# Lower products of an expert pair between gate and up of the next pair, with groups pinned in order and a branch hint

## The chip, the cores and the metric

The kernel runs on one core of one Trainium2 chip. The metric is the device time of one execution in microseconds. Smaller is better. Three executions of the kernel before gave 1344.26, 1339.33 and 1338.83 us, a median of 1339.33 us.

## What is computed

Two transformer blocks follow each other on 256 tokens of width 1024, all in float32. Each ends in a mixture of experts: every token goes to two experts, and each expert multiplies by three weight matrices.

```python
# first block: 16 experts of inner width 256
for e in range(N_EXPERTS):
    act = jax.nn.silu(t @ w_gate[e]) * (t @ w_up[e]) * gates[:, e:e + 1]
    y = y + act @ w_down[e]
...
# second block: 32 experts of inner width 512
for e in range(N_EXPERTS_2):
    a = jax.nn.silu(tok @ w_gate[e]) * (tok @ w_up[e])
    out = out + combine[:, e:e + 1] * (a @ w_down[e])
...
x = x + g2 * hier_moe_2(h2, ...)
return rms_norm_2(x, final_norm_g)
```

Between the two expert layers stands the mixer of the second block (projections, two scans, and their merge), which the change does not touch.

## The kernel before

`moe` (L937) is called twice, for 16 experts of width 256 (L1468, "first layer") and for 32 of width 512 (L1968, "second layer"). Experts are taken in **pairs**, which sit side by side on TensorE: each expert has 64 places for its tokens, and the two experts of a pair fill two halves of 64 columns. Four experts, two pairs, are a **quad**.

The steps of a pair, by the names of their PSUM tiles, are these. *gate*: 16 products into `pgg` (second layer) or the first half of `pgu` (first layer), with SiLU on ACT (`sgm`, L1159) and DVE (L1160). *up*: 16 products into `pgu`, then `act` on DVE (L1161). *turn* (L1165): transposes of `act` into `pactT`, copied to `actT` by ACT (L1170). *down* (L1173): the lower products into two tiles `pdn`, then `Pg`, `Ph`, `Pl` on DVE and ACT. *combine* (L1193): eight products `py` that add the pair into the sum `y`. Once for each quad *dispatch* (L1092) collects the tokens of the next quad: 32 products `pgx`, whose results ACT copies to `XT`, and then `pgt` and `pws`; `places` (L1085) makes its selection `Dd` on DVE just ahead.

In the loop (L1229 to L1247) `gate_up` runs gate and up of pair p; between the two, `half` (L1212) combines pair p-2 and turns pair p-1. Then `lower` (L1225) runs down of pair p-1, and `dispatch` follows at the end of a quad. The framework's scheduler sets the final order within each engine; `issue_after` pins an instruction behind another on its engine, and before the change only `half` of the first layer is pinned in the loop.

The weights come through one queue, SP, in the order that `Stream` writes (L504): gate and up of pair p, then down of pair p-1. Each load is 1024 KB, four for each matrix of a pair in the second layer and two in the first. A load needs a free buffer of a pool with 19 (`NG`), and it waits in SP's queue until the last product of the buffer's former tenant is done. `take` sets how far loads are written ahead (8 loads). The last two loads of the second layer are cut in halves (L534 to L542).

Behind the last pair every engine reads how many further chunks of tokens there are (`ns`, L1253), and branches past their code (`tc.If(ns > j)`, L1262). In these inputs no chunk is left, in either layer, and the branch is taken over the whole body.

Of the kernel before, what the change touches and what calls it, by code (L numbers as in the profile page):

```python
# [15 lines left out]
ALU = mybir.AluOpType  # L16
# [6 lines left out]
KD = 8  # L23
# [24 lines left out]
H1 = 1  # L48
# [74 lines left out]
def _body(es, tc, I, cst_d, msk_d, out_d, tap, stop):  # L123
# [380 lines left out]
    class Stream:  # L504
# [9 lines left out]
        def add_pair(self, a, b):  # L514
            p = len(self.ap)
            self.ap[p] = {k: (self.load(a, k), self.load(b, k)) for k in "gud"}
            keys = []
            for k in "gud":
                for i in range(len(self.ap[p][k][0])):
                    keys += [(p, k, 0, i), (p, k, 1, i)]  # L520
            gu = [q for q in keys if q[1] != "d"]
            d = [q for q in keys if q[1] == "d"]
            tail = self.order[len(self.order) - self.nd:] if self.order else []
            if p and self.n <= len(self.order) - len(tail):
                self.order[len(self.order) - len(tail):] = gu + tail + d
            else:
                self.order += gu + d
            self.nd = len(d)
# [16 lines left out]

        def take(self, p, kinds, look=8):
            want = [q for q in self.order if q[0] == p and q[1] in kinds]
            self.ahead(max(self.order.index(q) for q in want) + 1 + look)
            out = [[[self.t[(p, k, s, i)] for i in range(len(self.ap[p][k][s]))] for s in range(2)] for k in kinds]
            return out if kinds == "gu" else out[0]  # L550

# [384 lines left out]

    def moe(x, E, router, gcol, bcol, st, FE, n_static, mid=None, before_if=None, gate=None, idle=None):  # L937
        epg = E // 4
# [23 lines left out]
        y = [[ax_ps("py") for _ in range(2)] for _ in range(2)]  # L962
        if gate is not None:
# [70 lines left out]
        if gate is not None:  # L1034
# [57 lines left out]
        def dispatch(e0, n, xt=None, d=None, late=None):  # L1092
# [8 lines left out]
            for kk in range(4):  # L1101
# [6 lines left out]
                for j in range(2):  # L1108
                    k = 2 * kk + j
                    if late is not None and j:  # L1110
                        if bcol is None:
# [28 lines left out]

        def gate_up(gu, xt, off, wcol, half=None):
            act = W("act", [FE])
            if FE == 256:
                p = mm_ps("pgu", (2, 256))
                outs = [p[:, 0, :], p[:, 1, :]]
            else:
                outs = [mm_ps("pgg"), mm_ps("pgu")]
            for o, ws in zip(outs, gu):
                for k in range(KD):
                    for s in range(2):  # L1150
                        pc = ws[s]
                        per = KD // len(pc)
                        mm(o[64 * s:64 * s + 64, :], xt[:, k, off + 64 * s:off + 64 * s + 64], pc[k // per][:, k % per, :],
                           k == 0, k == KD - 1)
                if half:
                    half()
                    half = None
            sg = W("sgm", [FE])
            A.activation(sg, outs[0], AF.Sigmoid)  # L1159
            V.tensor_tensor(sg, sg, outs[0], op=ALU.mult)  # L1160
            V.scalar_tensor_tensor(act.rearrange("p (f c) -> p c f", f=NF), sg.rearrange("p (c f) -> p c f", f=NF), wcol,  # L1161
                                   outs[1].rearrange("p (c f) -> p c f", f=NF), op0=ALU.mult, op1=ALU.mult)
            return act

        def turn(act):  # L1165
            p = mm_ps("pactT", (NF, 128))
            for f in range(NF):
                PE.transpose(p[:, f, :], act[:, 128 * f:128 * f + 128], ident)
            aT = W("actT", [NF, 128])
            A.activation(aT, p, AF.Copy)  # L1170
            return aT

        def down(dn, aT):  # L1173
            parts = []
            for n in range(2):
                q = mm_ps("pdn")
                for f in range(NF):
# [4 lines left out]
                if gate is not None:  # L1182
                    qg = W("Pg", [512])
                    V.tensor_tensor(qg, q, gate[:, n, :], op=ALU.mult)  # L1184
                    q = qg
# [7 lines left out]
        def combine(parts, gt, first, final):  # L1193
            for n in range(2):
                for i in range(2):
                    for m in range(2):
                        mm(y[i][n], gt[:, 128 * i:128 * i + 128], parts[n][m], first and m == 0, final and m == 1)

# [10 lines left out]
        ei = spill()  # L1209
        acts, sums = [], []  # L1210

        def half():  # L1212
            with after(t2["mm"]) if E == 16 and H1 else nullcontext():
                if sums:
                    combine(*sums.pop(0))
                if acts:
                    acts[0][1] = turn(acts[0][1])

# [6 lines left out]
        def lower():  # L1225
            p, aT, gt = acts.pop(0)
            sums.append((down(st.take(p, "d"), aT), gt, p == 0 and gate is None, p == last - 1))

        for qi, e0 in enumerate(quads):  # L1229
            n = min(4, E + n_static - e0)  # L1230
            xt, gt, ws = nxt
            for a in range(n // 2):
# [6 lines left out]
                ahead = a == n // 2 - 1 and qi + 1 < len(quads)  # L1239
                if ahead:  # L1240
                    nn = min(4, E + n_static - e0 - 4)
                    d = places(e0 + 4, nn)
                if acts:
                    lower()
                if ahead:
                    nxt = dispatch(e0 + 4, nn, d=d)
                acts.append([p, act, gt[:, a, :]])  # L1247
        half()
        lower()
        half()  # L1250
        if before_if:
# [7 lines left out]
        def nest(j):  # L1259
            if j >= NSPILL:  # L1260
                return
            with tc.If(ns > j):  # L1262
                if not held:
# [4 lines left out]
                for k in "gud":  # L1268
                    out[k] = [[], []]
                    for i in range(len(aps[k][0])):  # L1270
                        for s in range(2):
# [6 lines left out]
                            q += 1  # L1278
                act = gate_up([out["g"], out["u"]], xt, 0, ws[:, 0:1])
                combine(down(out["d"], turn(act)), gt[:, 0, :], False, True)  # L1280
# [686 lines left out]

    y = moe(x3, 32, rt, mod2q, sh2q, st2, 512, 0, gate=gf[0], idle=last_ada)  # L1968
    ss = S("sf", [2, 2], bufs=1)
# [41 lines left out]
```

## Time and profile before

| | us |
|---|---|
| median of three executions | 1339.33 |
| the profiled execution | 1341.91 |
| its span, first to last instruction | 1340.14 |
| first expert layer, first gate product to last combine | 174.4 to 316.0 |
| second expert layer, first gate product to last combine | 862.9 to 1325.8 |

The profile is one execution. Busy time is not speed: a matmul is pipelined, so the next one starts before the modelled end of the last, and the pace of a group is read from the starts of the groups. "PE" is TensorE's products, "PEq" its sequencer. The idle time in square brackets is that of the engine just before the row, with what ended it. The trace counts each float32 product of 512 or 256 columns of gate, up and down as two instructions, so 16 products are 32 there.

### The profile page before, as it was taken

To read this page: it belongs to the slowest core of one execution; us is meant where nothing else is said; L and a number is where in the kernel's file an instruction comes from. 1 tells how busy PE (TensorE), PEld (TensorE's weight loads), DVE (VectorE), ACT (ScalarE), POOL (GpSimd) and SP (SyncE) were. 2 spreads that over 40 slices of the span, in tenths; PEclk is the share of its full clock that TensorE was granted. 3 is DMA by queue.
4 is the path that set the end of the run, shared out by engine and by line. 5 is a ranking of instruction groups with operands and counts; after the bars stand their busy time and mean duration, and the time that the engine had idled before them with its cause. 6 is when DMAs were issued, how large, how long until landed. Compare 5 with 4: busy or idle time off the path is not lost. (4 is left out here: it accounts for less than half of the span.)

```text
span 1340.1 us, 19921 instructions
## 1 busy us (share of the span) xinstructions
PE 1278.2 (95%) x8098; PEld 842.5 (63%) x8098; DVE 647.4 (48%) x1416; ACT 437.5 (33%) x756; POOL 38.7 (3%) x50
## 2 busy tenths in 40 slices
PE   6988999998999999999999999899999999999995
PEld 5845466666788998898988988643434334343431
DVE  6895541115479988876565765821111111211113
ACT  5734322223234655554344443310201111110102
POOL 4110100000000000000000000100000000000000
PEclk9989999998999999999999999899999999999998
DMA  8698789963423231342516677699999999999990
GB/s 272 232 338 316 253 333 380 410 282 117 153 82 95 77 112 50 114 131 81 164 44 206 228 263 286 238 422 421 422 422 422 422 421 421 422 422 422 421 391 33
DMA packets 124356, 359.81 MB, mean 268 GB/s; under 512 B 15272, under 2 KB 64593, under 8 KB 97632
## 3 DMA queue, kind: packets, MB, share of 16 engines
q1 hardware_dynamic: 114224, 355.49, 69.8%
q10 hardware_dynamic: 9024, 2.24, 0.8%
q8 instruction: 68, 1.11, 0.3%
q0 software_dynamic: 1008, 0.70, 0.2%
q14 instruction: 32, 0.26, 0.1%
HBM read 357.35 MB, written 1.05 MB: 267 GB/s over the span
## 5 line engine op out<-in xcount | busy, mean ns | idle before, releaser
L156 PE MATMUL pg<-hT,hi 128*128 128x256 f32 (+1 forms) x1024 | 232.7, 321 | 1.5 <-DVE Qg L1352 1.5
L156 PE MATMUL pgu<-w,XT 128*64 128x256 f32 (+1 forms) x1088 | 190.3, 481 | 0.0
L156 PE MATMUL pdn<-w,actT 128*64 128x512 f32 x656 | 180.6, 596 | 0.5 <-ACT actT L1170 0.5
L156 PEld LDWEIGHTS pg<-hT,hi 128*128 128x128 f32 x1024 | 167.2, 188 | 16.3 <-DVE Qg L1352 1.7
L236 DVE TENSOR_TENSOR lo<-w,hi 128x1024 fp32r<-128x1024 f32 x122 | 146.0, 1219 | 49.6 <-ACT hi L235 21.5
L156 PE MATMUL pg<-hT,lo 128*128 128x256 f32 (+1 forms) x512 | 162.3, 317 | 0.0
L235 ACT ACTIVATE hi<-w 128x1024 fp32r<-128x1024 f32 x122 | 125.0, 1053 | 93.4 <-PE pr L156 32.1
L156 PEld LDWEIGHTS pgu<-w,XT 128*64 128x64 f32 x1088 | 81.3, 137 | 92.2 <-issue 71.4
L156 PE MATMUL pgg<-w,XT 128*64 128x512 f32 x512 | 127.1, 596 | 0.0
L156 PEld LDWEIGHTS pdn<-w,actT 128*64 128x64 f32 x656 | 56.0, 137 | 93.9 <-issue 85.7
L156 PEld LDWEIGHTS pg<-hT,lo 128*128 128x128 f32 x512 | 96.2, 188 | 7.4 <-issue 0.4
L156 PE MATMUL pr<-hi,hT 128*128 128x256 f32 (+1 forms) x384 | 90.6, 326 | 3.7 <-PEq L1262 3.7
L156 PEld LDWEIGHTS pgg<-w,XT 128*64 128x64 f32 x512 | 37.8, 137 | 70.5 <-issue 68.7
L1184 DVE TENSOR_TENSOR Pg<-pdn,g 128x512 f32<-128x512 f32 x32 | 22.1, 689 | 117.5 <-PE pdn L156 117.3
L1160 DVE TENSOR_TENSOR sgm<-sgm,pgg 128x512 f32<-128x512 f32 x16 | 11.0, 688 | 130.6 <-ACT sgm L1159 130.6
L1188 ACT ACTIVATE Ph<-Pg 128x512 fp32r<-128x512 f32 x32 | 20.1, 629 | 163.5 <-DVE Pg L1184 163.5
L156 PEld LDWEIGHTS pr<-hi,hT 128*128 128x128 f32 x384 | 65.2, 191 | 10.5 <-issue 4.1
L1161 DVE SCALAR_TENSOR_TENSOR act<-sgm,ws,pgu 128x512 f32<-128x512 f32 (+1 forms) x25 | 23.8, 952 | 87.2 <-PE pgu L156 86.8
L156 PE MATMUL pr<-lo,hT 128*128 128x256 f32 (+1 forms) x192 | 62.6, 326 | 0.0
L1119 ACT ACTIVATE XT<-pgx,adaq,mod2q 128x256 f32<-128x256 f32 x60 | 30.0, 562 | 96.3 <-PE pgx L156 96.3
L156 PE MATMUL pgx<-Dd,xnh 128*128 128x256 f32 (+1 forms) x208 | 53.0, 295 | 3.9 <-DVE Dd L1089 3.8
L156 PEld LDWEIGHTS pgx<-Dd,xnh 128*128 128x128 f32 x208 | 40.3, 195 | 20.4 <-issue 13.7
(520 smaller groups left out, 1920.0 us busy)
## 6 DMA issues: line engine op xcount, KB each, us to landing
w<-in_w_gate_dram SPq DMA_DIRECT2D x82, 1024.0 KB, 16.5
w<-in_w_up_dram SPq DMA_DIRECT2D x82, 1024.0 KB, 12.6
w<-in_w_down_dram SPq DMA_DIRECT2D x80, 1024.0 KB, 16.3
w<-in_w_in_dram SPq DMA_DIRECT2D x98, 512.0 KB, 4.5
w<-in_w_ada_dram SPq DMA_DIRECT2D x24, 1024.0 KB, 6.4
w<-in_w_out_dram SPq DMA_DIRECT2D x4, 1024.0 KB, 5.2
w<-in_w_branch_b_dram SPq DMA_DIRECT2D x8, 512.0 KB, 4.5
w<-in_w_branch_a_dram SPq DMA_DIRECT2D x8, 512.0 KB, 4.6
```

The lines of the kernel that those rows point to most:

```text
L156: t2["mm"] = PE.matmul(out, lhsT, rhs, start=start, stop=stop, skip_group_check=True)
L235: t2["hi"] = A.activation(hi[:, ks], t, AF.Copy)
L236: t2["lo"] = V.tensor_tensor(lo[:, ks], t, hi[:, ks].bitcast(F32), op=ALU.subtract)
L1119: A.activation(xt[:, k, 0:w], p[:, j, :], AF.Identity, scale=gcol[:, k:k + 1], bias=bcol[:, k:k + 1])
L1160: V.tensor_tensor(sg, sg, outs[0], op=ALU.mult)
L1161: V.scalar_tensor_tensor(act.rearrange("p (f c) -> p c f", f=NF), sg.rearrange("p (c f) -> p c f", f=NF), wcol, outs[1].rearrange("p (c f) ...
L1184: V.tensor_tensor(qg, q, gate[:, n, :], op=ALU.mult)
L1188: A.activation(ph, q, AF.Copy)
```

## The change

`gate_up` is split into `gate` and `up`, with their common loop in `up_to`. `lower` turns pair p-1 and runs its down between gate and up of pair p, and combine of pair p-1 follows up of pair p. Gate, up, turn, the first half of down, combine and dispatch are each pinned behind the product issued last before them. Down's loads move from behind up to between gate and up, and `take` writes 12 loads ahead in the second layer and 10 in the first. In the second layer every dispatch, not only the first, gives every second `XT` copy to DVE. Combine's loops change places, so that both products with `Ph` stand ahead of those with `Pl`. A hint on TensorE's queue ahead of the last turn names the branch at `ns` as likely taken. The argument `gate` of `moe` becomes `gain`.

```diff
         def add_pair(self, a, b):
...
-            gu = [q for q in keys if q[1] != "d"]
-            d = [q for q in keys if q[1] == "d"]
+            g, u, d = ([q for q in keys if q[1] == k] for k in "gud")
...
-                self.order[len(self.order) - len(tail):] = gu + tail + d
+                self.order[len(self.order) - len(tail):] = g + tail + u + d
...
-        def take(self, p, kinds, look=8):
...
+            self.ahead(max(self.order.index(q) for q in want) + 1 + (12 if n > 1 else 10))
...
-                    if late is not None and j:
+                    if (late is not None or E == 32) and j:
...
+        def gate(w, xt, off):
...
+            with after(t2["mm"]):
+                up_to(outs[0], w, xt, off)
             sg = W("sgm", [FE])
             A.activation(sg, outs[0], AF.Sigmoid)
             V.tensor_tensor(sg, sg, outs[0], op=ALU.mult)
+            return sg, outs[1]
...
         def turn(act):
             p = mm_ps("pactT", (NF, 128))
-            for f in range(NF):
-                PE.transpose(p[:, f, :], act[:, 128 * f:128 * f + 128], ident)
+            with after(t2["mm"]):
+                for f in range(NF):
+                    tr = PE.transpose(p[:, f, :], act[:, 128 * f:128 * f + 128], ident)
+            t2["mm"] = tr
...
         def lower():
-            p, aT, gt = acts.pop(0)
-            sums.append((down(st.take(p, "d"), aT), gt, p == 0 and gate is None, p == last - 1))
+            p, a, gt = act
+            return down(st.take(p, "d"), turn(a)), gt, p == 0 and gain is None, p == last - 1
...
-                act = gate_up(st.take(p, "gu"), xt, 128 * a, ws[:, a:a + 1], half if p else first)
...
+                sg, o = gate(st.take(p, "g"), xt, 128 * a)
+                parts = None
+                if act:
+                    parts = lower()
+                else:
+                    first()
+                act = [p, up(st.take(p, "u"), xt, 128 * a, sg, o, ws[:, a:a + 1]), gt[:, a, :]]
...
+                    if parts:
+                        combine(*parts)
+                    with after(t2["mm"]):
+                        nxt = dispatch(e0 + 4, nn, d=d)
...
-        half()
-        lower()
-        half()
+        with after(t2["mm"]):
+            tc.mark_branch_hint_location("spill%d" % E, "LikelyTaken", engines=[mybir.EngineType.PE])
+        combine(*lower())
...
-            with tc.If(ns > j):
+            with tc.If(ns > j, label="spill%d" % E if j == n_static else None):
```

TensorE's queue in the middle of the second layer before, from down of one pair to the next but one (`pdn` down, `py` combine, `pactT` turn):

```order
L156 MATMUL pdn<-w,actT 64x512 x16
L156 MATMUL py<-Ph,Gt 128x512 x2
L156 MATMUL py<-Pl,Gt 128x512
L156 MATMUL pgg<-w,XT 64x512
L156 MATMUL py<-Pl,Gt 128x512
L156 MATMUL py<-Ph,Gt 128x512 x2
L1168 MATMUL pactT<-cst,act 128x128 x2
L156 MATMUL py<-Pl,Gt 128x512 x2
L1168 MATMUL pactT<-cst,act 128x128 x2
L156 MATMUL pgg<-w,XT 64x512 x15
L156 MATMUL pgu<-w,XT 64x512 x16
L156 MATMUL pdn<-w,actT 64x512 x2
```

Combine and turn are mixed with the first product of gate (`pgg`), and down stands behind up (`pgu`). The same place after the change, one pair:

```order
L156 MATMUL pgg<-w,XT 64x512 x16
L1175 MATMUL pactT<-cst,act 128x128 x4
L156 MATMUL pdn<-w,actT 64x512 x16
L156 MATMUL pgu<-w,XT 64x512 x16
L156 MATMUL py<-Ph,Gt 128x512 x2
L156 MATMUL py<-Pl,Gt 128x512 x2
L156 MATMUL py<-Ph,Gt 128x512 x2
L156 MATMUL py<-Pl,Gt 128x512 x2
```

Each group stands in one piece, and down has moved from behind up to just behind the turn.

TensorE's queue at the end of the second layer before, from up of the last pair on:

```order
L156 MATMUL pgu<-w,XT 64x512 x16
L156 MATMUL pdn<-w,actT 64x512 x2
L1168 MATMUL pactT<-cst,act 128x128 x4
L156 MATMUL pdn<-w,actT 64x512 x14
L156 MATMUL py<-Ph,Gt 128x512 x2
L156 MATMUL py<-Pl,Gt 128x512 x2
L156 MATMUL py<-Ph,Gt 128x512 x2
L156 MATMUL pdn<-w,actT 64x512
L156 MATMUL py<-Pl,Gt 128x512 x2
L156 MATMUL pdn<-w,actT 64x512 x15
L156 MATMUL py<-Ph,Gt 128x512 x2
```

Both last downs stand behind up of the last pair. The same place after the change, from gate of the last pair:

```order
L156 MATMUL pgg<-w,XT 64x512 x16
L1175 MATMUL pactT<-cst,act 128x128 x4
L156 MATMUL pdn<-w,actT 64x512 x16
L156 MATMUL pgu<-w,XT 64x512 x16
L156 MATMUL py<-Ph,Gt 128x512 x2
L156 MATMUL py<-Pl,Gt 128x512 x2
L156 MATMUL py<-Ph,Gt 128x512 x2
L156 MATMUL py<-Pl,Gt 128x512 x2
L2018 BRANCH_PREFETCH_HINT
L1175 MATMUL pactT<-cst,act 128x128 x4
L156 MATMUL pdn<-w,actT 64x512 x16
L156 MATMUL py<-Ph,Gt 128x512 x2
```

Down of the last pair but one has moved ahead of up of the last pair, and the hint stands ahead of the last turn.

ACT's queue in the second layer before, from the dispatch of a quad on (`sgm` sigmoid, `actT` the copy of a turn):

```order
L1170 ACTIVATE actT<-pactT 128x512
L1159 ACTIVATE sgm<-pgg 128x512
L1188 ACTIVATE Ph<-Pg 128x512 x2
L1170 ACTIVATE actT<-pactT 128x512
L1159 ACTIVATE sgm<-pgg 128x512
L1119 ACTIVATE XT<-pgx,adaq,mod2q 128x256 x8
```

A turn's copy stands ahead of the sigmoid of the next pair, and all eight `XT` copies are ACT's. The same place after the change:

```order
L1119 ACTIVATE XT<-pgx,adaq,mod2q 128x256 x4
L1158 ACTIVATE sgm<-pgg 128x512
L1178 ACTIVATE actT<-pactT 128x512
L1197 ACTIVATE Ph<-Pg 128x512 x2
L1158 ACTIVATE sgm<-pgg 128x512
```

The sigmoid has moved ahead of the copy, and four of the eight `XT` copies have left this queue.

## Rows read from the trace of the kernel before

**Rows 1.** The page: tenths busy, granted clock and DMA in 40 slices of 33.5 us
```profile
PE   6988999998999999999999999899999999999995
...
PEclk9989999998999999999999999899999999999998
DMA  8698789963423231342516677699999999999990
```

**Rows 2.** Stretches: us; busy PE, PEld, DVE, ACT, POOL (instructions); clock; DMA share; GB/s
```profile
880.00:1300.00 420.00, 413.22 (x1876) 167.54 (x1874) 74.64 (x120) 62.87 (x114) 0.00 (x0) 1.00 1.01 422
1300.00:1326.00 26.00, 23.78 (x90) 8.26 (x86) 6.44 (x9) 3.01 (x5) 0.00 (x0) 1.00 0.18 70
```

**Rows 3.** The same view: one quad of the second expert layer
```profile
1004.50:1063.82 59.32, 58.08 (x263) 23.47 (x260) 10.53 (x17) 8.91 (x16) 0.00 (x0) 1.00 1.01 421
```

**Rows 4.** Timeline, PE: start, length, line, what; groups in one piece
```profile
899.50 0.39 PE L156 MATMUL pgx<-Dd,xnh 128*128 128x256 f32 x1
...
903.37 0.40 PE L156 MATMUL py<-Ph,Gt 128*128 128x512 f32 x1
...
905.20 0.60 PE L1129 MATMUL pgt<-cst,Dd 128*128 128x128 f32 x4
...
906.52 7.09 PE L156 MATMUL pgg<-w,XT 128*64 128x512 f32 x32
913.54 0.66 PE L1168 MATMUL pactT<-cst,act 128*128 128x128 f32 x4
914.12 7.09 PE L156 MATMUL pgu<-w,XT 128*64 128x512 f32 x32
921.04 7.04 PE L156 MATMUL pdn<-w,actT 128*64 128x512 f32 x32
```

**Rows 5.** Timeline, PE: a piece of a lower product, first and second layer
```profile
286.79 3.65 PE L156 MATMUL pdn<-w,actT 128*64 128x512 f32 x12
...
1008.36 3.65 PE L156 MATMUL pdn<-w,actT 128*64 128x512 f32 x12
```

**Rows 6.** DMA from 1250 to 1340 us in 40 slices of 2.25 us
```profile
GB/s 415 422 415 422 419 422 422 430 422 426 422 426 415 422 415 426 415 422 426 422 408 413 406 326 169 0 0 0 7 0 0 0 0 4 7 7 0 0 313 153
```

**Rows 7.** Timeline: the end of the second layer, on PE, DVE and ACT
```profile
1314.62 7.09 PE L156 MATMUL pdn<-w,actT 128*64 128x512 f32 x30
...
1322.98 0.68 DVE L1184 TENSOR_TENSOR Pg<-pdn,g 128x512 f32<-128x512 f32 x1
...
1325.11 0.73 PE L156 MATMUL py<-Pl,Gt 128*128 128x512 f32 x2
1329.05 0.60 ACT L1973 ACTIVATE rj<-py 128x512 f32<-128x512 f32 x1 [4.72 <-PEq L1262]
```

**Rows 8.** Timeline: a turn with nothing behind it; a sigmoid on ACT
```profile
310.16 3.65 PE L156 MATMUL pdn<-w,actT 128*64 128x512 f32 x16 [0.47 <-ACT actT L1170]
...
1294.90 0.60 ACT L1159 ACTIVATE sgm<-pgg 128x512 f32<-128x512 f32 x1 [6.41 <-PE pgg L156]
```

**Rows 9.** Timeline behind the first branch (L1262): DVE and PE
```profile
319.48 2.48 DVE L1472 TENSOR_TENSOR x<-x,py 128x512 f32<-128x512 f32 x4 [4.31 <-PEq L1262]
319.65 0.77 PE L156 MATMUL pr<-hi,hT 128*128 128x512 f32 x1 [3.68 <-PEq L1262]
...
328.77 3.73 PE L156 MATMUL ptr<-rdg,x 128*128 128x128 f32 x32
```

**Rows 10.** DMA, 315.97 to 319.65 in 40 slices; one packet, queue q8 instruction
```profile
GB/s 0 0 0 0 0 0 0 0 0 178 0 0 0 0 0 0 0 0 0 0 0 0 0 0 0 0 0 0 0 0 0 0 0 0 0 0 0 0 0 0
```

**Rows 11.** Busy time by stretch: two of the stretches at the lower clock
```profile
86.31:93.13 6.82, 4.49 (x16) 1.75 (x15) 5.84 (x26) 5.08 (x21) 0.00 (x0) 0.50 1.02 377
...
318.41:325.24 6.83, 5.59 (x13) 4.51 (x14) 5.40 (x21) 1.69 (x5) 0.00 (x0) 0.50 0.39 114
```

**Rows 12.** Timeline, PE: two idles early in the kernel
```profile
85.28 1.60 PE L156 MATMUL psc<-qkT 64*128 64x128 f32 x8 [3.23 <-DVE ex L844]
...
104.82 0.66 PE L617 MATMUL pac<-cst,adap 128*128 128x128 f32 x4 [1.31 <-ACT adap L614]
```

More of the change, by code (lines that the diff above doesn't have):

```diff
@@ L544, in ahead, with take @@
                 self.n += 1
-        def take(self, p, kinds, look=8):
[L547 to L550, printed above, removed]
+        def take(self, p, k):
+            n = len(self.ap[p][k][0])
+            want = [q for q in self.order if q[0] == p and q[1] == k]
+            self.ahead(max(self.order.index(q) for q in want) + 1 + (12 if n > 1 else 10))
+            return [[self.t[(p, k, s, i)] for i in range(n)] for s in range(2)]
     def wsel(w, e):
@@ L934, in _body, with moe @@
         return
-    def moe(x, E, router, gcol, bcol, st, FE, n_static, mid=None, before_if=None, gate=None, idle=None):
+    def moe(x, E, router, gcol, bcol, st, FE, n_static, mid=None, before_if=None, gain=None, idle=None):
         epg = E // 4
@@ L962, in moe @@
         y = [[ax_ps("py") for _ in range(2)] for _ in range(2)]
-        if gate is not None:
+        if gain is not None:
             with after(plg):
@@ L1033, in moe @@
                                        q4(xh[0][:, cs].bitcast(F32), 1), op0=ALU.mult, op1=ALU.subtract)
-        if gate is not None:
+        if gain is not None:
             with after(pos):
@@ L1139, in dispatch, with up_to @@
             return xt, gt, ws
-        def gate_up(gu, xt, off, wcol, half=None):
-            act = W("act", [FE])
+        def up_to(o, ws, xt, off):
+            for k in range(KD):
+                for s in range(2):
+                    pc = ws[s]
+                    per = KD // len(pc)
+                    mm(o[64 * s:64 * s + 64, :], xt[:, k, off + 64 * s:off + 64 * s + 64], pc[k // per][:, k % per, :],
+                       k == 0, k == KD - 1)
+        def gate(w, xt, off):
             if FE == 256:
@@ L1146, in gate_up @@
             else:
[L1147 to L1155, printed above, removed]
-                    half()
-                    half = None
+                outs = [mm_ps("pgg"), None]
+            with after(t2["mm"]):
+                up_to(outs[0], w, xt, off)
             sg = W("sgm", [FE])
@@ L1176, in down @@
                 q = mm_ps("pdn")
-                for f in range(NF):
+                with after(t2["mm"]) if n == 0 else nullcontext():
+                  for f in range(NF):
                     for s in range(2):
@@ L1181, in down @@
                            pc[f // 2][:, f % 2, 512 * n:512 * n + 512], f == 0, f == NF - 1)
-                if gate is not None:
+                if gain is not None:
                     qg = W("Pg", [512])
-                    V.tensor_tensor(qg, q, gate[:, n, :], op=ALU.mult)
+                    V.tensor_tensor(qg, q, gain[:, n, :], op=ALU.mult)
                     q = qg
@@ L1193, in combine @@
         def combine(parts, gt, first, final):
-            for n in range(2):
-                for i in range(2):
+            with after(t2["mm"]):
+                for n in range(2):
                     for m in range(2):
-                        mm(y[i][n], gt[:, 128 * i:128 * i + 128], parts[n][m], first and m == 0, final and m == 1)
+                        for i in range(2):
+                            mm(y[i][n], gt[:, 128 * i:128 * i + 128], parts[n][m], first and m == 0, final and m == 1)
         def ex(e):
@@ L1209, in moe @@
         ei = spill()
[L1210 to L1217, printed above, removed]
+        act = None
         def first():
@@ L1278, in nest @@
                             q += 1
-                act = gate_up([out["g"], out["u"]], xt, 0, ws[:, 0:1])
+                sg, o = gate(out["g"], xt, 0)
+                act = up(out["u"], xt, 0, sg, o, ws[:, 0:1])
                 combine(down(out["d"], turn(act)), gt[:, 0, :], False, True)
@@ L1966, in last_ada @@
         yield
-    y = moe(x3, 32, rt, mod2q, sh2q, st2, 512, 0, gate=gf[0], idle=last_ada)
+    y = moe(x3, 32, rt, mod2q, sh2q, st2, 512, 0, gain=gf[0], idle=last_ada)
     ss = S("sf", [2, 2], bufs=1)
```

21 lines of the change are left out of this document (11 added, 10 removed).

## The prediction, made before the changed kernel ran

> **What bounds the kernel now.** I read the page first: TensorE is busy in nearly every slice, and from the 27th slice on the DMA engines are full too [rows 1]. A share of 95% does not say which of the two sets the end, so the second layer was split into stretches. From 880 to 1300 us the DMA runs at 422 GB/s with a share of 1.01, so it has no hole at all, while PE counts 413 of 420 us as busy [rows 2]. Then comes the point on which most hangs: the DMA's slices show the last weights landing by 1306.25 us (25 slices of 2.25 us from 1250) [rows 6], and the last combine ends at 1325.11 + 0.73 = 1325.84 us [rows 7]. So PE runs 19.6 us behind its weights at the end. The two are nearly matched: a quad has 24 loads of 1.0486 MB, and 25.17 MB at 422 GB/s are 59.6 us, against 59.32 us between the same point of two quads on PE [rows 3]. PE starts the layer behind a filled store of buffers, and at that pace it wins back only 0.3 us a quad. The end of the layer is PE's, with the DMA close beneath.
>
> In the first layer PE is at 9 tenths in slices 7 to 9, and it ends it at 315.97 us. Behind each layer stands a gap at the branch: 3.68 us on PE and 4.31 us on DVE after the first layer [rows 9], 3.2 us from PE's last product to ACT's first square after the second (1325.84 to 1329.05) [rows 7].
>
> **Groups in one piece, second layer.** Early in this layer the groups stood in one piece already, and their pace can be read from the starts [rows 4]: gate 913.54 - 906.52 = 7.02, turn 0.58, up 6.92, down 7.04 at most (its length), combine 1.83, `pgx` 903.37 - 899.50 = 3.87, `pgt` and `pws` 1.32 us. A quad in one piece is 2 x (7.02 + 0.58 + 6.92 + 7.04 + 1.83) + 3.87 + 1.32 = 52.0 us. The quad as it runs later takes 59.32 [rows 3], 7.3 us more: 12 instructions of down as a separate piece take 3.65 us [rows 5] where 12/32 of 7.04 is 2.64, and there are several such pieces in each quad, besides waits for `Dd` and `Pl`. Pinning removes the pieces, and up covers `Pg`, `Ph`, `Pl`.
>
> **The new wait.** The turn now stands directly ahead of the down that needs its copy. Queued behind that wait on PE are down, up and combine of the pair, so nothing covers it. The one place before where a turn has nothing behind it waits 0.47 us, with a copy of half the size [rows 8]: the low end. The high end is a full sigmoid of 0.60 us [rows 8], which now stands ahead of the copy on ACT, and a copy of the same shape, some 0.1 us of handover, with nothing beside it: 1.3 us. The transposes (0.58 us) run beside the sigmoid, so I take 0.8. A quad is then 52.0 + 1.6 = 53.6 us, 6 us under the DMA's 59.6.
>
> So PE catches up. The gate that began at 906.52 us is that of the third pair; seven quads less one dispatch and a last turn, down and combine end near 907 + 7 x 53.6 - 5 + 10 = 1287 us, if weights were there. They are not: the layer becomes bound by loads. I keep the loads where they were, since the DMA had no hole and its order only changes inside a pair. After 1306.25 us PE still has 20 of down's 32 instructions (the last quarter of its first half, and its second half): 20/32 of 7.04 = 4.4 us, and then the chain from `Pg` to the last `py`, 1325.84 - 1322.98 = 2.9 us [rows 7], with 0.3 us for handovers. That ends at 1313.8: **12.0 us earlier**. Bounds: 6 us (the tail at half clock, below) and 13 us.
>
> **First layer.** The same wait is paid 8 times, with a sigmoid and copy of half the columns: 0.47 us at the low end, 0.9 at the high; I take 0.65, 5.2 us. All of it is on the path, since PE is the bound there. Against it stand pieces of down mixed with `pgx` and up near the end of that layer: one costs 1.0 us [rows 5], and with the other pieces up to 3; I take 2.5. Net **+2.7 us**, between +0.8 and +6.
>
> **The hint.** Between PE's last product (315.97 us) and the release of DVE (319.48 us) [rows 9] one packet moves, from an instruction queue, in the tenth of 40 slices of 0.092 us, at 316.8 [rows 10]. So some 0.9 us pass ahead of the fetch, and 2.6 us are fetch and what follows. The hint's own cost has no row; ahead of the last turn lie 5 us of other products. I take 2.5 us gained at the first branch (0 if it does nothing, 3.5 if all goes). The gap also lowered the clock: from 318.41 to 325.24 us PE had 0.50, and 5.59 us of products [rows 11], which at full clock are 2.8. Those products, until `ptr` at 328.77 [rows 9], are PE's alone, and the DVE chain to `ptr` starts from the same release, so **2.5 + 2.8 = 5.3 us** go, and the mixer behind it moves up whole: its slices are full on PE, not on DMA. The remaining idle is about 1.2 us; one of 1.31 us left the clock up, and one of 3.23 us lowered it [rows 11, 12]. At the end of the second layer the same fetch gives **2.0 us** (0 to 3.2), since DVE and ACT branch too and have no hint.
>
> By the Trainium skill, "Runtime: NRT & Kernel Launch", section Instruction fetch mechanics, prefetch is purely sequential, and a taken branch out of the fetched window forces a fetch. The trace shows such a fetch [rows 10]. By that sentence alone a hint would bring nothing, which is the first rival.
>
> Other edits cost nothing: combine's loop order is the one that the trace shows already, DVE has room for four copies a quad (74.6 of 420 us busy, ACT 62.9) [rows 2], and loads written 12 ahead stay within the store of buffers.
>
> **Sum.** Against the profiled execution of 1341.91 us: -12.0 + 2.7 - 5.3 - 2.0 = -16.6, so 1325.3. That execution lies 2.6 us above the median of 1339.33, and from the median the forecast is **1322.7 us**.
>
> **Rivals.**
> - *The hint does nothing.* Both fetches and the low clock behind the first stay: + 5.3 + 2.0, 1330 us. For it: nothing in the trace shows a hint. Against: the fetch takes 1 us of a 3.5 us gap, and there are 5 us to do it in.
> - *The waits for loads lower the clock.* Once PE has caught up, it waits up to 3 us where down needs its second two loads (2 x 2.5 us) after 1.7 us of products. Idles of 3.2 and 3.7 us each brought 6.8 us at half clock [rows 11, 12]. One costs 3.4 us of PE's time, less than the 6 us a quad has to spare; it counts only in the last 7 us, and there costs up to 6: 1329 us.
> - *The turn holds PE as the bound.* It would need 24 us more over 14 turns, 2.5 us each instead of 0.8. With a wait of 2.5 us in the first layer as well, that gives 1322.7 + 12 + 15 = about 1345; with it in the second alone, 1334.
> - *Slower: the DMA runs dry.* Loads wait in SP's queue for a buffer, and a down now frees its four late or early relative to the gate and up around it. If the engines stood still 0.5 us at each of the 48 groups of four loads, the layer would end 24 us later, 1347 us; from 0.35 us a group (17 us) the change is no gain. Against it: no hole in 420 us with 8 loads written ahead [rows 2], and 12 now.
>
> **How the numbers follow.** The forecast (1317 to 1327) 0.55; no hint 0.17; low clock in the tail 0.10; turns as the bound 0.07; DMA dry 0.07; better than 1317 0.04. The range, 1316 to 1332, takes in the first three cases. A measurement of this kernel tells about 0.5% from no change, 6.7 us: faster, under 1332.6, 0.84; within it 0.09; slower, over 1346, 0.07.
>
> **What would show it.** Right: quads of the second layer at 59.6 us with PE idle before gate, up and down until a load lands, from about the middle of the layer on; the last combine 7 to 8 us behind the last load; an idle of 0.8 us on PE ahead of each down in the second layer and 0.65 in the first, ended by `actT`; an idle near 1.2 us behind the first branch and no half clock there. Wrong: a DMA share under 1 in the second layer, PE ending it without waits for loads, or the 3.7 us at the branch still there.

## The result, and the profile after

The changed kernel took 1325.26, 1328.45 and 1325.86 us; against the kernel before (four executions, median 1340.13 us) that is a ratio of 0.9891, with a 95% interval of 0.9873 to 0.9909, or about 14.6 us less. A fourth execution of the changed kernel took 6838.44 us, at a granted clock of 0.169, and is left out as a slow one. A second measurement on another chip gave 0.9898 (0.9882 to 0.9915). The forecast was 1322.7 us, in a range of 1316 to 1332. The profiled execution took 1325.26 us with a span of 1323.4, 16.7 us less than the profiled execution of before; the sum had -16.6.

The page of the changed kernel: tenths busy on PE, granted clock, and DMA in 40 slices of 33.1 us.

```profile
PE   6988999999999999999999999899999998999895
...
PEclk9989899999999999999999999899999999999998
DMA  8798799983533241352525676799999999999993
```

Beside [rows 1] little seems to have changed, and the DMA is as full as before. What changed is who waits. The waits of PE from 860 to 1312 us, the second expert layer (total, times, longest in us):

```profile
PE pdn L156 <- ACT actT L1178: 11.1, 16, 0.7
PE pgu L156 <- DMA w<-in_w_up_dram: 10.6, 8, 1.4
...
PE pgg L156 <- DMA w<-in_w_gate_dram: 1.1, 1, 1.1
```

PE now waits for weights of gate and up, from 1093.81 us on. Before, PE waited for no load in this layer; from 862 to 1326 us its largest wait in total was for `Pl`:

```profile
PE py L156 <- DVE Pl L1189: 3.4, 6, 0.6
```

The stretches of [rows 2] and a late quad, between the same wait of two up groups (columns as there):

```profile
880.00:1300.00 420.00, 397.16 (x1908) 185.76 (x1906) 93.08 (x153) 52.27 (x89) 0.00 (x0) 1.00 1.01 421
1168.26:1227.90 59.64, 55.61 (x260) 25.66 (x260) 12.60 (x21) 7.08 (x13) 0.00 (x0) 1.00 1.01 422
```

The quad takes 59.64 us, which is 24 loads at 422 GB/s. Only 2.6 us of PE's waiting for loads in it stand as idle, ahead of and within one up. The rest is inside the groups: for instance, one gate lasts 7.93 us and one up 7.84 in place of 7.09, as the products of one expert of the pair run alone for a while. Earlier in the layer, while the stored buffers still covered it, PE went at its own pace. PE's timeline there, one quad from down to down:

```profile
1018.58 7.19 PE L156 MATMUL pdn<-w,actT 128*64 128x512 f32 x32 [0.69 <-ACT actT L1178]
...
1072.17 3.33 PE L156 MATMUL pdn<-w,actT 128*64 128x512 f32 x14 [0.69 <-ACT actT L1178]
```

That is 53.59 us, where the prediction had 53.6. The first branch (PE's last combine, DVE's and PE's first work behind it, and `ptr`, as [rows 9]):

```profile
316.88 0.64 PE L156 MATMUL py<-Pl,Gt 128*128 128x512 f32 x2
317.92 2.48 DVE L1483 TENSOR_TENSOR x<-x,py 128x512 f32<-128x512 f32 x4 [1.29 <-PEq L1272]
318.09 0.47 PE L156 MATMUL pr<-hi,hT 128*128 128x512 f32 x1 [0.57 <-PEq L1272]
...
324.70 3.73 PE L156 MATMUL ptr<-rdg,x 128*128 128x128 f32 x32
```

PE's gap is 0.57 us in place of 3.68. And the end of the second layer, where DMA fell silent at 1302.0 us (the layer's last loads in slices of 0.2 us from 1298):

```profile
GB/s 410 369 430 328 328 266 266 287 246 205 287 246 184 205 225 225 164 184 184 41 0 0 0 0 0 0 0 0 0 0 0 0 0 0 0 0 0 0 0 0
```

```profile
1299.55 7.14 PE L156 MATMUL pdn<-w,actT 128*64 128x512 f32 x32 [0.75 <-ACT actT L1178]
1306.71 0.69 DVE L1193 TENSOR_TENSOR Pg<-pdn,g 128x512 f32<-128x512 f32 x1 [9.21 <-PE pdn L156]
...
1308.77 0.68 DVE L1193 TENSOR_TENSOR Pg<-pdn,g 128x512 f32<-128x512 f32 x1
...
1310.17 1.11 PE L156 MATMUL py<-Ph,Gt 128*128 128x512 f32 x2 [0.53 <-ACTq L1272]
1311.08 1.05 PE L156 MATMUL py<-Pl,Gt 128*128 128x512 f32 x2
1312.31 0.60 ACT L1984 ACTIVATE rj<-py 128x512 f32<-128x512 f32 x1 [2.20 <-PEq L1272]
```

The last combine ends at 1312.13 us, 10.1 us behind the last load (before: 19.6), and ACT begins 0.18 us later (before: 3.2).

To compare all runs by stage, the table takes five points from the timeline of each profiled execution: the first gate product and the end of the last combine of both layers, and ACT's first square at the end. The last load is read from DMA slices of 0.2 us (0.25 for the kernel before). All in us.

| run | first layer | branch and mixer | second layer | combine to ACT | first gate to last load | last load to last combine |
|---|---|---|---|---|---|---|
| before | 141.6 | 546.9 | 462.9 | 3.2 | 443.4 | 19.6 |
| changed | 144.5 | 541.4 | 453.2 | 0.2 | 443.1 | 10.1 |
| changed, again | 144.4 | 541.5 | 453.3 | 0.2 | 443.2 | 10.0 |
| no hint | 144.3 | 545.3 | 453.4 | 3.0 | 443.3 | 10.2 |
| hint alone | 141.6 | 543.3 | 463.0 | 0.3 | 443.3 | 19.7 |
| twofold turns | 144.4 | 541.2 | 454.2 | 0.2 | 443.6 | 10.7 |
| early turn | 140.4 | 542.1 | 453.4 | 0.2 | 443.4 | 10.0 |
| no pins | 146.3 | 542.0 | 476.7 | 0.2 | 443.1 | 33.6 |
| old order, pinned | 139.0 | 543.6 | 453.3 | 3.2 | 443.3 | 9.9 |
| the same and hint | 139.0 | 542.5 | 453.1 | 0.2 | 443.2 | 9.9 |
| old loads | 144.7 | 541.3 | 457.4 | 0.2 | 443.0 | 14.4 |
| early turn, other end | 140.3 | 542.1 | 450.6 | 0.2 | 443.2 | 7.5 |
| old order, other end | 139.0 | 541.7 | 453.2 | 0.2 | 443.3 | 9.9 |
| copies on ACT | 144.4 | 541.0 | 453.5 | 0.2 | 443.3 | 10.2 |

The sixth column says most: the last load lands 443.0 to 443.6 us behind the first gate in every run, whatever PE does. What differs in the second layer is how far PE ends behind it.

### The profile page after: what moved, and what is told of

It reads as the page before. It is cut to its first block, busy times and chain, and to the rows that moved or that the text cites. A ratio compares the mean times of both kernels' runs of the same rounds, so it can differ in the third digit from the quotient of the medians.

```text
span 1323.4 us, 19929 instructions
## 1 busy us (share of the span) xinstructions
PE 1248.6 (94%) x8098; PEld 852.8 (64%) x8098; DVE 662.1 (50%) x1444; ACT 424.9 (32%) x728; POOL 38.5 (3%) x50
## 5 line engine op out<-in xcount | busy, mean ns | idle before, releaser
L156 PE MATMUL pgu<-w,XT 128*64 128x256 f32 (+1 forms) x1088 | 185.9, 481 | 10.6 <-DMA w<-in_w_up_dram 10.6
L236 DVE TENSOR_TENSOR lo<-w,hi 128x1024 fp32r<-128x1024 f32 x122 | 146.0, 1218 | 44.6 <-ACT hi L235 16.6
L156 PE MATMUL pdn<-w,actT 128*64 128x512 f32 x656 | 153.3, 597 | 15.6 <-ACT actT L1178 15.6
L156 PEld LDWEIGHTS pgu<-w,XT 128*64 128x64 f32 x1088 | 87.7, 137 | 102.2 <-issue 61.2
L156 PE MATMUL pgg<-w,XT 128*64 128x512 f32 x512 | 117.1, 596 | 1.1 <-DMA w<-in_w_gate_dram 1.1
L1158 ACT ACTIVATE sgm<-pgg 128x512 f32<-128x512 f32 x16 | 9.6, 597 | 176.6 <-PE pgg L156 176.6
L156 PE MATMUL pgx<-Dd,xnh 128*128 128x256 f32 (+1 forms) x208 | 49.5, 283 | 0.1
L156 PE MATMUL pgx<-Dd,xnl 128*128 128x256 f32 (+1 forms) x208 | 49.3, 282 | 0.0
## 6 DMA issues: line engine op xcount, KB each, us to landing
w<-in_w_up_dram SPq DMA_DIRECT2D x82, 1024.0 KB, 19.7
```

Source lines behind the costliest of these rows:

```text
L156: t2["mm"] = PE.matmul(out, lhsT, rhs, start=start, stop=stop, skip_group_check=True)
L236: t2["lo"] = V.tensor_tensor(lo[:, ks], t, hi[:, ks].bitcast(F32), op=ALU.subtract)
```

## The experiments

### Does the hint close the gaps?

```diff
-        with after(t2["mm"]):
-            tc.mark_branch_hint_location("spill%d" % E, "LikelyTaken", engines=[mybir.EngineType.PE])
```

> The changed kernel without the branch hint; nothing else differs. Theory (the hint starts the fetch of the code behind the branch early): the gap of 3.7 us on PE behind the first layer comes back in place of 0.57 us, with some 6.8 us at half clock behind it, together 5.6 us; at the end ACT starts 3.2 us after the last combine in place of 0.18 us, 3.0 us. The time rises by 8.6 us, to a ratio of about 0.9955 against the kernel before. Rival (the hint does nothing, and the gaps closed because the groups before the branch now stand in another order): gaps as in the changed kernel, and a ratio of 0.989.

Ratio 0.9938 (0.9914 to 0.9962). PE's first product behind the first branch, and ACT's start at the end:

```profile
320.43 0.74 PE L156 MATMUL pr<-hi,hT 128*128 128x512 f32 x1 [3.37 <-PEq L1270]
```

```profile
1318.79 0.60 ACT L1982 ACTIVATE rj<-py 128x512 f32<-128x512 f32 x1 [5.14 <-PEq L1270]
```

Both gaps are back, so the hint closes them and not the order of the groups. The span is 6.5 us longer, some 2 us short of what was expected; about half of that is clock, as less of it was lost behind the gap (below). The other way round, the kernel before was given the hint alone, ahead of the last down:

```diff
         half()
+        with after(t2["mm"]):
+            tc.mark_branch_hint_location("spill%d" % E, "LikelyTaken", engines=[mybir.EngineType.PE])
         lower()
...
-            with tc.If(ns > j):
+            with tc.If(ns > j, label="spill%d" % E if j == n_static else None):
```

> The kernel before with the hint alone, written ahead of the last lower products of each layer; order, pinning and loads are those of before. Theory: 5.6 us at the first branch and 3.0 us at the second go, 8.6 us, a ratio of 0.9936; the second layer is as long as before. Rival (the hint does nothing by itself): 1.000.

Ratio 0.9924 (0.9902 to 0.9946). PE behind the first branch, and ACT at the end:

```profile
316.30 0.47 PE L156 MATMUL pr<-hi,hT 128*128 128x512 f32 x1 [0.68 <-PEq L1264]
```

```profile
1322.21 0.60 ACT L1975 ACTIVATE rj<-py 128x512 f32<-128x512 f32 x1 [1.84 <-PEq L1264]
```

The gaps close in the old kernel too, and both layers are as long as before (141.6 and 463.0 us). The rival that a hint does nothing has fallen. Where the fetch went is seen in the DMA slices: without the hint, from 308 to 321 us in slices of 0.325, one transfer stands alone at 317.4 us, just behind the last combine (317.06); with it, from 308 to 320 in slices of 0.3, none stands between 312.8 and 318.5 us, and PE is at work again from 318.09. Two packets of the instruction queue q8 are counted in each stretch; in shorter stretches, the one that stood behind the last combine is found between 311 and 313 us with the hint, beside loads. The first view is of the run without the hint, the second of the changed kernel. The third is of the kernel before with the hint alone, from 308 to 321 in slices of 0.325, where no loads hide it: the packet stands at 309.95 us, 5.7 us ahead of the end of the last combine (315.63).

```profile
GB/s 315 403 384 233 107 69 126 296 353 309 202 82 32 0 0 0 0 0 25 0 0 0 0 0 0 0 0 0 0 50 0 0 0 0 0 0 0 0 0 50
...
q8 instruction: 2, 0.03, 1.1%
```

```profile
GB/s 198 328 396 382 266 89 137 82 225 369 321 253 212 123 41 14 0 0 0 0 0 0 0 0 0 0 0 0 0 0 0 0 0 0 0 55 0 0 0 0
...
q8 instruction: 2, 0.03, 1.2%
```

```profile
GB/s 0 0 0 0 0 0 50 0 0 0 0 0 0 0 0 0 0 0 0 0 0 0 0 0 0 0 50 0 0 0 0 0 25 82 113 246 340 309 370 281
```

### Is the second layer bound by its loads?

First, more work on PE: the transposes of a turn made twice.

```diff
-                for f in range(NF):
+                for f in list(range(NF)) * (2 if E == 32 else 1):
```

> The changed kernel with the four transposes of a turn made twice in the second layer (the second time over the first, same values): 0.58 us more on PE for each of 16 pairs. Theory (bound by loads): PE waits for loads for 0.58 us less at each pair of the later quads; only the last turns, behind the last loads of up, add to the time: 0.6 to 1.2 us, a ratio of 0.990. Rival (PE is the bound of the second layer): 16 x 0.58 = 9.3 us more, a ratio of 0.996.

Ratio 0.9883 (0.9861 to 0.9905). The second layer is 1.0 us longer with 9.3 us of added products, of which the last turn's 0.6 us was expected. Then less waiting on PE: the turn in the middle of the next gate, which covers the copy.

```diff
             with after(t2["mm"]):
-                up_to(outs[0], w, xt, off)
+                up_to(outs[0], w, xt, off, range(4))
+            aT = turn(act[1]) if act else None
+            with after(t2["mm"]):
+                up_to(outs[0], w, xt, off, range(4, KD))
```

> The changed kernel with the turn of a pair between the first and the second half of the next pair's gate, so that half of gate covers the copy to actT. Theory (the second layer is bound by its loads, the first by PE): the 8 or 9 idles of 0.47 to 0.53 us in the first layer go, 4.2 us; those of 0.69 us in the second layer go too, but PE then waits for loads instead; the last turn is not covered. 4 us less than the changed kernel, a ratio of 0.986. Rival (the turns hold PE as the bound in both layers): 4.2 + 15 x 0.69 = 14.5 us less, a ratio of 0.978.

Ratio 0.9866 (0.9839 to 0.9893). The first layer is 4.1 us shorter, the second the same to 0.2 us. Its waits on PE from 855 to 1309 us:

```profile
PE pgu L156 <- DMA w<-in_w_up_dram: 15.3, 14, 1.4
PE pdn L156 <- DMA w<-in_w_down_dram: 2.7, 5, 0.6
...
PE pdn L156 <- ACT actT L1181: 0.7, 1, 0.7
```

The 11.1 us of waits for `actT` are down to the last one, and loads are waited for instead, 18.0 us in place of 11.7. Work added and waits removed on PE both leave the layer as it is, to 1.0 us: it is bound by its loads.

### Pins or order: what made the groups whole?

The changed kernel without its pins:

```diff
-            with after(t2["mm"]):
-                up_to(o, w, xt, off)
+            up_to(o, w, xt, off)
```

(gate, turn, down, combine and dispatch likewise.)

> The changed kernel without the pins on gate, up, turn, down, combine and dispatch; written order, loads and hint stay. Theory (the pins keep the groups whole): combine stands in pieces among up again, a quad takes 55 us or more, PE catches up with its loads later or not at all, 5 to 12 us more than the changed kernel, a ratio of 0.993 to 0.998. Rival (the written order alone is enough, and bound by loads PE has room for the pieces): a ratio of 0.989.

Ratio 1.0078 (1.0062 to 1.0093): slower than the kernel before, and by more than either theory allowed. One quad on PE, from its first gate to that of the next quad:

```profile
1142.93 7.09 PE L156 MATMUL pgg<-w,XT 128*64 128x512 f32 x32
...
1170.80 0.66 PE L1172 MATMUL pactT<-cst,act 128*128 128x128 f32 x4 [1.18 <-DVE act L1165]
1171.39 7.08 PE L156 MATMUL pgg<-w,XT 128*64 128x512 f32 x30
1179.70 7.14 PE L156 MATMUL pdn<-w,actT 128*64 128x512 f32 x32 [1.24 <-ACT actT L1175]
1187.45 0.73 PE L156 MATMUL py<-Ph,Gt 128*128 128x512 f32 x2 [0.61 <-ACT Ph L1194]
...
1188.61 1.07 PE L156 MATMUL pgu<-w,XT 128*64 128x512 f32 x2
1189.61 0.50 PE L156 MATMUL py<-Pl,Gt 128*128 128x512 f32 x1
...
1204.59 7.09 PE L156 MATMUL pgg<-w,XT 128*64 128x512 f32 x32
```

A quad takes 61.66 us, above the 59.6 of the loads, so PE stays the bound to the end and falls behind by 2 us a quad. Pieces are there again: a piece of two instructions of up lasts 1.00 us (1188.61 to 1189.61), where 2 of the 32 in a whole group take 0.44. The rows show why. Two instructions are one product, so one expert of the pair alone. An instruction lasts 0.59 to 0.64 us and both together 1.07, so the second starts 0.48 us behind the first; in a whole group, 32 in 7.09 us, one starts every 0.21 us, as the products of the two experts run side by side. The scheduler has parted a product from its partner, and alone it runs at half the pace. The piece in [rows 5] is of this kind too: its 12 instructions last as long as 16 in one piece [rows 8], since 8 of them start in pairs and 4 alone. But waits weigh as much: they are 5.8 us of this quad, against 1.4 in a quad of the changed kernel at PE's own pace. The scheduler set the turn ahead of gate, where `act` is not there yet (1.18 us), and combine ahead of up, where `Ph` is not (0.61 us). In the written order each of these had cover only while it stood where it was written.

The pins without the order, in the kernel before (no hint either):

```diff
             for o, ws in zip(outs, gu):
+                with after(t2["mm"]):
                   for k in range(KD):
...
-            with after(t2["mm"]) if E == 16 and H1 else nullcontext():
-                if sums:
-                    combine(*sums.pop(0))
-                if acts:
-                    acts[0][1] = turn(acts[0][1])
+            if sums:
+                combine(*sums.pop(0))
+            if acts:
+                acts[0][1] = turn(acts[0][1])
...
+                    with after(t2["mm"]):
                         nxt = dispatch(e0 + 4, nn, d=d)
```

(turn, down and combine are pinned inside, and combine's loops change places, as in the changed kernel.)

> The kernel before, in its own order (gate, combine of p-2 and turn of p-1, up, down of p-1) and with its own loads, but with every group pinned behind the one before it, in both layers; no hint. Theory (whole groups alone make the second layer bound by its loads, and the move of down between gate and up is not needed): no idle ahead of down, since up covers the turn; PE waits for loads in the second layer, and the last combine ends about 8 us behind the last load, 12 us earlier than before; 2.5 us less in the first layer; both gaps at the branches stay. A ratio of 0.989. Rival (the move is what wins the time, since down right behind up waits for its loads or combine for its operands): the second layer is as long as before, a ratio of 0.998 to 1.000.

Ratio 0.9900 (0.9883 to 0.9917), without the hint as fast as the changed kernel with it. Its waits on PE from 858 to 1345 us:

```profile
PE pgg L156 <- DMA w<-in_w_gate_dram: 12.7, 9, 2.3
PE pdn L156 <- DMA w<-in_w_down_dram: 3.2, 6, 0.7
```

The second layer takes 453.3 us, as in the changed kernel, and the first 139.0 us, 5.5 less than there, for the most part since up covers the turn. With the hint added in the same way as above:

> The run with the old order and pinned groups, with the hint ahead of the last down of each layer. Theory (pins and hint are the whole gain, the move of down costs the turn's idle in the first layer): 7 to 8.6 us less than with the pins alone, so a ratio of 0.984 to 0.985, some 5 us less than the changed kernel. Rival (the move of down gives something beside the pins, which the pinned old order lacks): no better than the changed kernel, 0.989.

Ratio 0.9866 (0.9849 to 0.9882), against 0.9898 for the changed kernel on the same chip. That is some 4 us less; the first theory's figure lies at the edge of the interval, the rival's outside. So the move of down behind gate gave nothing that pins in the old order don't give, and it costs the first layer 5.5 us. The hint gave 5.2 us of span here in place of 8.6. The clock accounts for 2.5 us of the difference: behind the gap of the run with the pins alone there was no low clock to win back. Beside that, branch and mixer became only 1.1 us shorter though the gap shrank by 2.8, as with the hint PE waited 2.0 us more in the mixer, for `Dd` (1.2 us) and for `adap` (0.8); and the first gate came 1.0 us earlier. The cause of these two is not shown. Stretches with busy time, granted clock (the third number from the end) and DMA, first of the run with the pins alone, its gap and the products behind it up to `ptr`, then of the run without the hint, the first products behind its gap of 3.37 us:

```profile
313.44:316.95 3.51, 0.00 (x1) 0.03 (x1) 0.17 (x1) 0.00 (x0) 0.00 (x0) 1.00 0.02 5
316.95:323.51 6.56, 6.56 (x28) 5.34 (x29) 6.12 (x27) 2.51 (x5) 0.00 (x0) 1.00 0.56 150
```

```profile
320.43:324.00 3.57, 3.57 (x9) 2.85 (x10) 3.57 (x10) 1.45 (x4) 0.00 (x0) 0.52 0.26 58
```

An idle of 3.51 us left the clock at 2.4 GHz, and one of 3.37 us was followed by 3.57 us at 0.52, so some 3.4 us at 1.2 GHz.

### The order of the loads, and other edits

```diff
-                self.order[len(self.order) - len(tail):] = g + tail + u + d
+                self.order[len(self.order) - len(tail):] = g + u + tail + d
```

> The changed kernel with the old order of loads, gate and up of p ahead of down of p-1 (still written 12 and 10 ahead). Theory (bound by loads; the order inside a pair counts only at the end): the quads stay at 59.6 us; at the end down of the last pair but one waits for the last loads but four, and up, combine, turn and down of the last pair follow it, so that the last combine ends some 4.5 us later: a ratio of 0.9925. Rival (the order of loads does nothing, PE is late at the end anyway): 0.989. In the first layer, bound by PE, neither expects a change.

Ratio 0.9926 (0.9910 to 0.9943). The quads keep the pace of the loads, and PE waits for down (16.8 us in all, 3.3 at the longest) in place of up. The last combine ends 14.4 us behind the last load, 4.3 more than in the changed kernel. The end on PE and DVE:

```profile
1306.80 7.09 PE L156 MATMUL pdn<-w,actT 128*64 128x512 f32 x32 [0.75 <-ACT actT L1178]
1310.53 0.69 DVE L1193 TENSOR_TENSOR Pg<-pdn,g 128x512 f32<-128x512 f32 x1 [5.78 <-PE pdn L156]
...
1313.94 0.69 DVE L1193 TENSOR_TENSOR Pg<-pdn,g 128x512 f32<-128x512 f32 x1 [1.27 <-PE pdn L156]
...
1316.08 0.73 PE L156 MATMUL py<-Pl,Gt 128*128 128x512 f32 x2
```

Here the first `Pg` starts in the middle of down, and the last combine ends 2.9 us behind down's end (1313.89 to 1316.81); in the changed kernel both `Pg` stand behind down, and it takes 5.4. There the first `Pg` waits for `pdn` to the end of down, so the two halves of the last down end together; why they do is not shown.

The copies to `XT` back on ACT (`if late is not None and j:`):

> The changed kernel with all copies to XT on ACT in the second layer, as in the kernel before. Theory (bound by loads): dispatch takes up to 1 us longer in a quad, PE's waits for loads get shorter by that, and the time is that of the changed kernel, 0.989. Rival (the copies on ACT hold up the dispatch and thereby the gate by more than the loads leave room for): 0.993 and above.

Ratio 0.9891 (0.9875 to 0.9907), as the changed kernel on the same chip:

> The changed kernel once more, on the chip of these runs, as the measure for them: a ratio of 0.989, within 0.002. Its second expert layer should be bound by loads again, 59.6 us between the same waits of two late quads, and its last combine 10 us behind its last load.

Ratio 0.9898 (0.9882 to 0.9915). The same waits of two late quads lie 59.88 and 59.59 us apart (1167.67, 1227.55 and 1287.14 us), and the last combine ends 10.0 us behind the last load.

### A version faster than the changed kernel

With the second layer bound by loads, what is left is its end and the turns of the first layer. The early turn is kept; at the end of the second layer up of pair 15 goes ahead of down of pair 14 (its loads too), the turn of pair 15 between the halves of that down, the last down takes its products in the order of its loads, and both combines follow, which fill the wait for DVE and ACT.

```diff
+                if E == 32 and p == E // 2 - 1:
+                    prev, act = act, [p, up(st.take(p, "u"), xt, 128 * a, sg, o, ws[:, a:a + 1]), gt[:, a, :]]
+                    aL = []
+                    pa = down(st.take(p - 1, "d"), aT, lambda: aL.append(turn(act[1])))
+                    break
...
+        if E == 32:
+            pb = last_down(st.take(act[0], "d"), aL[0])
+            combine(pa, prev[2], False, False)
+            combine(pb, act[2], False, True)
```

> The changed kernel with the turn inside the next gate, as in the run with the early turn, and another end of the second layer: the last four loads but four are those of down of pair 14, as in the old order; up of pair 15 stands ahead of down of pair 14, the turn of pair 15 between the halves of that down, and the last down follows with its products in the order of its loads, then both combines; on DVE both products with the gain stand ahead of both differences. Theory: 4 us less than the changed kernel by the turns, and the last combine 6 us behind the last load in place of 10, 4 us more: a ratio of 0.983. Rival (at the end PE stands still so long that the clock drops, which eats the gain): 0.986, as with the early turn alone.

Ratio 0.9842 (0.9821 to 0.9862), 1319.63 us against 1340.99. That is faster than the changed kernel, but the interval overlaps those of the early turn alone and of the pinned old order with the hint; that the other end gives something is seen in the stages, with a second layer of 450.6 us in place of 453.4. The end on PE:

```profile
1294.85 10.57 PE L156 MATMUL pdn<-w,actT 128*64 128x512 f32 x48
...
1305.35 0.73 PE L156 MATMUL py<-Ph,Gt 128*128 128x512 f32 x2
...
1308.66 0.61 PE L156 MATMUL py<-Pl,Gt 128*128 128x512 f32 x2
```

From the turn of pair 15 (1294.26 us) on PE has no idle, and the combine ends 7.5 us behind the last load, where 6 were expected. The same end in the pinned old order, with combine of pair 14 ahead of the last down:

> The same with another end of the second layer: the turn of pair 15 between the halves of down of pair 14, the last down in the order of its loads, and on DVE both products with the gain ahead of both differences. Theory (the end lies behind the last load: rest of down, then the chain on DVE and ACT): the last combine 6 us behind the last load in place of 7.9, a ratio of 0.983. Rival (the end is set by something else): the same as without, 0.9845.

Ratio 0.9851 (0.9838 to 0.9864), not to be told from the run without it (0.9866). The last combine ends 9.9 us behind the last load, as there (not 7.9, as the expectation has it):

```profile
1297.68 0.73 PE L156 MATMUL py<-Ph,Gt 128*128 128x512 f32 x2 [0.35 <-ACT Ph L1212]
...
1299.07 7.09 PE L156 MATMUL pdn<-w,actT 128*64 128x512 f32 x32
1306.84 1.28 PE L156 MATMUL py<-Ph,Gt 128*128 128x512 f32 x3 [0.68 <-ACT Ph L1189]
```

The chain behind down became 1 us shorter (1306.16 to 1309.29), but down itself starts later: 0.3 us before the last load (1299.07 against 1299.4), where without the other end it began 1.3 us before it (1296.85 against 1298.2). The one eats the other, and the rival was right.

## Why the prediction was right

**The second layer became bound by its loads: shown.** The quad at PE's own pace took 53.59 us (forecast 53.6), the late quad 59.64 (forecast 59.6), and two opposite experiments on PE's work changed the layer's length by 1.0 and 0.2 us. The idle ahead of down was 0.69 to 0.75 us (forecast 0.8), so the rival that the turn holds PE as the bound has fallen. The DMA share was 1.01 from 880 to 1300 us, so the one of a DMA that runs dry has too. PE's first wait for a load came at 1093.81 us, in the middle of the layer, as forecast. The forecast put the gain by whole groups down to the pieces; their price, 1.0 us for each in [rows 5], is that of products parted from their partners.

**The end of the second layer: the term was too large by 2.3 us.** The layer became 9.7 us shorter, not 12.0. The last load landed 443.1 us behind the first gate, as before, and the rest of down took 4.7 us (forecast 4.4). What failed is the chain behind it: I took 2.9 us from the second `Pg` on [rows 7], though the first `Pg` came only 0.8 us ahead of down's end (1321.71) in that trace too:

```profile
1320.92 0.69 DVE L1184 TENSOR_TENSOR Pg<-pdn,g 128x512 f32<-128x512 f32 x1 [7.96 <-PE pdn L156]
```

From it to the end of the last combine were 4.9 us; in the changed kernel they were 5.4 (1306.71 to 1312.13), all behind down, so that the last combine ended 10.1 us behind the last load and not 7 to 8. Where the halves of down end one after the other, as with the old loads, it is the 2.9 us that I had taken. The clock, a rival with up to 6 us, took the 0.5 between 4.9 and 5.4: from 1310 us on it was at 0.54, and the last four products took 1.96 us from start to end (1310.17 to 1312.13) in place of 1.46.

**First layer: +2.9 us, forecast +2.7, by terms that hold, and one that it lacked.** Nine idles of 0.47 to 0.54 us make 4.5 us (forecast 8 of 0.65), and hiding eight of them gave 4.1 back. The gain by whole groups alone was 2.6 us with the pinned old order (141.6 to 139.0; forecast 2.5). These two leave 1.0 us of the +2.9. Most of it is a wait in the first pair, which neither the kernel before nor the pinned old order has:

```profile
178.68 0.63 PE L617 MATMUL pac<-cst,adap 128*128 128x128 f32 x4 [0.76 <-DVE Gt L1131]
```

**The hint: right, and larger.** From the end of the first layer to the first gate of the second 5.5 us went (forecast 5.3): 3.1 in the gap and 2.5 by the clock, as `ptr` starts 6.61 us behind the first product and not 9.12. At the end 3.0 us went, not 2.0: one hint on PE's queue was enough, as ACT's start hangs on PE's sequencer before and after [rows 7]. By the Trainium skill, "Runtime: NRT & Kernel Launch", section Instruction fetch mechanics, a taken branch out of the fetched window forces a fetch. Without the hint the traces agree, with gaps of 3.4 to 3.7 us. The same section of the Trainium skill calls prefetch purely sequential. There the runs differ: with the hint the gap is 0.5 to 0.7 us, and a packet of the instruction queue moves ahead of the branch.

**The sum came out by chance as well.** The stages add up to -15.3 us (+2.9 - 5.5 - 9.7 - 3.0); the first gate of this execution also came 1.4 us earlier, in a part that the change doesn't touch. By the ratio the gain is 14.6 us, and the median of 1325.86 us lies 3.2 above the forecast.

**What the prediction did not see.** It took the change as a whole and never asked whether down had to move. It had to be pinned only. The old order, pinned, has the same second layer and a first layer 5.5 us shorter.

## What to carry to other kernels

Where loads and PE are nearly matched, compare the landing of the last load with the end of the last product: as long as the loads stay as they are, the difference is the most that any work on PE can win (19.6 us here), and once PE waits for loads, only the work behind the last load counts. Write groups in an order in which each wait has cover, and pin that order; the same written order without pins took 25 us longer here. At a branch that is taken over a long body, a hint on the engine that the others wait for is worth a try: here it closed a gap of 3 us at each of two branches.

## What was not expected of the hardware

- The length of an idle of PE alone does not tell whether the clock falls: at the branch, 3.37 us was followed by some 3.4 us at 1.2 GHz and 3.68 us by 6.8 us [rows 11], while 3.51 us was followed by none. So the price of such a gap, beyond its own length, was 0 to 2.6 us.
- Nine waits for loads of 1.1 to 1.4 us in the changed kernel's second layer left the granted clock at 1.00 from 880 to 1300 us. With the old order of loads, one of 2.51 us (to 1046.06) left it at 1.00, but behind one of 2.25 us (to 1225.59) it was 0.61 for 4.41 us, and behind one of 3.30 us (to 1106.61) 0.64 for 4.39 us.
- A piece of two instructions of up takes 1.00 us, where its share of a whole group is 0.44 us: the partner with which it runs side by side in the group stands elsewhere.
